# Moving window sums and squares from GpSimd to VectorE, with four plain gate tiles and weights first, in a four-layer fp32 trunk

## The chip, the cores and the metric

The kernel runs on one core of a Trainium2 chip. The metric is the device time of one execution in microseconds. Before the change it is 1521.63 us, the median of three runs (1519.23 to 1524.7).

## The reference

Four pre-norm residual layers over x (512 tokens, 1024 channels, fp32): pool, conv, latent attention (MLA), pool, and a closing RMSNorm. What matters here is the pool layer, and that every product has to be exact to fp32.

```python
POOL_WINDOWS = (2, 4, 8, 16)            # one per group of 512 of the 2048 inner channels

def pool_mixer(xn, w_in, w_grp, scale, w_out):
    u, z = split(xn @ w_in, 2)          # 1024 -> 2 x 2048
    for g, w in enumerate(POOL_WINDOWS):
        mean = (c - prev) / minimum(count_base, w)   # trailing mean of u over w tokens
        pooled.append(mean - u[g])
    mixed = einsum(pooled, w_grp) * scale            # 512 x 512 for each group
    return (mixed * silu(z)) @ w_out                 # 2048 -> 1024

def mla_mixer(...):
    q_lat, kv_lat, k_rope, z = split(xn @ w_in)      # 384, 256, 64, 2048
    q = rms_norm(q_lat) @ w_q_up                     # 16 heads x (128 + 64)
    kv = rms_norm(kv_lat) @ w_kv_up                  # 16 heads x (128 + 128)
    o = causal softmax attention(q, kv, rotated k_rope)
    return (o * silu(z)) @ w_out

for i in range(4):                                   # pool, conv, mla, pool
    x = x + mixer(rms_norm(x), ...)
return rms_norm(x, final_norm)
```

## The kernel before

x lies on the chip as 8 tiles of 128 channels by 512 tokens. A number is held as a high and a low part, each of 32 bits, and a product is three matmuls (high by high, low by high, high by low; lines L257 to L259). Weights come by DMA as raw tiles `wr` of 128x1024 and are split by two steps: `wh` on ScalarE (L244) and `wl` on VectorE (L247). With `pool=True` both stand on GpSimd (L242, L247); that is used for the weights of attention's heads.

Work is a list of **jobs** in a `Stream`. A plain tile (`Layer.tile`, `u..`) is 24 matmuls of 512 columns; a pair (`Layer.pair`, `seven`, `z..`) gives two output tiles at once from sums and differences of weights and of x, with 84 matmuls of 256 columns, and needs eight weight parts in place of four (`ah`, `al`, `sh`, `sl`, `ch`, `cl`, `th`, `tl`; `al`, `sl`, `cl` and `tl` are made on VectorE, L395). The job `m..` mixes a group's channels (24 matmuls), `h0` and `h1` are the halves of the out-projection (tiles `o`). The digits of `u12` are group and tile; `z01` is group 0, second pair. The order of the jobs of the first pool layer is written out by hand:

```python
ORDER = ("u00 u01 u02 u03 u10 u11 u12 u13 z00 z01 m00 m01 z10 z11 " + LATE, ...)
```

While job j runs its matmuls, positions 0 to 7 are counted, and other steps are put at these positions in lists: `prepare(j + 1)`, the weight splits of the next job (a plain tile at positions 1 and 2, a pair at 4 to 7 and 10, 11, where 8 and more means the next job); the post steps of the product before (`post_u`, `post_z`); the forms of x (`XNorm.forms`, the sums and differences that a pair needs, L356 to L381); and sums of squares (`Stats.add`, L281). `Steps.put` (L171) appends, so at one position what was put first goes first. Within `Stream.run` the instructions of TensorE, VectorE and ScalarE stand in exactly this written order, in one in-order queue for each engine. Attention and the first part of the second pool layer lie outside `run`, and there a scheduler sets the order by its own estimates.

`post_u` multiplies a u tile by R (the norm's factor, one row for each token), then makes the trailing sum over w tokens by 1 to 4 shifted adds (`s<-u`, then `s<-s`, 128x513 to 128x527, L608) on GpSimd, then on VectorE the mean and its difference to u (`mean`, three instructions, L615 to L617) at position 12, the high part at 14 on ScalarE and the low part `pll` at 16 on VectorE. A first small memset of the 16 padding columns is GpSimd's (L602). GpSimd also adds squares of x for the norms (L281, all but a layer's last), scales the probabilities p in attention (L1021), and starts some DMAs.

`first_two`, at the end of the kernel, runs u00 and u01 while x still arrives, and R of the first layer comes late: the products up to u11 wait for it in PSUM, and their post steps are drawn into the jobs that follow, up to z00.

## Time and profile before

| what | value |
|---|---|
| median of three runs | 1521.63 us |
| profiled execution | 1516.26 us, span 1514.4 us |
| TensorE, mean granted clock | 0.984 |
| TensorE busy | 1455.7 us (96%), 8632 matmuls |
| VectorE busy | 1096.8 us (72%) |
| ScalarE busy | 677.9 us (45%) |
| GpSimd busy | 324.9 us (21%) |
| DMA | 183.30 MB, mean 121 GB/s |

All times of the trace count from the start of the span of the profiled execution. That execution took 1516.26 us, 5.4 us less than the median of the three runs. A row of the timeline names the start, the length shown, engine, line, operation and the tiles as out<-in; what stands in brackets is the idle time before it and what ended that. The length shown of a VectorE instruction holds some 0.08 us that overlaps with the next one, so the distance of two starts is the better price where instructions follow each other without a wait. In the table of stretches, idle time of an engine is the length less its busy time; PEclk is the granted clock of TensorE as a share of its upper level.

### The profile page before, as it was taken

The page shows a single profiled execution, that of the slowest core. Times are in us where ns is not written, and L with a number is a line of the kernel's source. Part 1 is how long each engine was busy: PE and PEld are TensorE (multiplying, and loading weights), DVE is VectorE, ACT ScalarE, POOL GpSimd, SP SyncE. Part 2 cuts the span into 40 slices and gives each one's busy share as a digit, 9 for nine tenths or more (in the row PEclk, how much of TensorE's full clock was granted, in tenths as well). Part 3 has the DMA queues.
Part 4 walks back from the last instruction along what each step waited for, and adds up shares of the span by engine and source line. Part 5 has one row for each costly group of instructions (what it writes and reads, how often), then busy time and mean ns, then how long its engine had stood idle before and what let it go on. Part 6 is the DMA issues. An engine that isn't in the chain of part 4 may idle for free.

```text
span 1514.4 us, 22602 instructions
## 1 busy us (share of the span) xinstructions
PE 1455.7 (96%) x8632; PEld 1281.9 (85%) x8632; DVE 1096.8 (72%) x1757; ACT 677.9 (45%) x1170; POOL 324.9 (21%) x337
## 2 busy tenths in 40 slices
PE   9799999999999999999989998999999999999997
PEld 7698797887999899999869977888888798888886
DVE  7985557659989879998778867666655487755854
ACT  5353242445555335554455644444633354323333
POOL 2502206021000000000211014355501122310602
PEclk9899999999999999999999999999999999999999
DMA  6353354325676366665236641222122434333431
GB/s 218 89 136 119 88 149 98 126 84 121 180 194 174 126 148 182 173 188 174 84 90 170 169 130 37 69 70 84 43 84 84 111 107 110 129 101 114 123 112 56
DMA packets 66012, 183.30 MB, mean 121 GB/s; under 512 B 8176, under 2 KB 8176, under 8 KB 65904
## 3 DMA queue, kind: packets, MB, share of 16 engines
q1 hardware_dynamic: 57264, 151.97, 31.2%
q0 software_dynamic: 7776, 28.32, 11.4%
q10 hardware_dynamic: 864, 1.57, 0.3%
q8 instruction: 68, 1.11, 0.3%
q14 instruction: 40, 0.33, 0.1%
HBM read 175.27 MB, written 2.10 MB: 117 GB/s over the span
## 4 chain that ended last, share of the span: by engine, by line
PE 68%; DVE 16%; DMA 4%; issue 4%; ACT 4%; POOL 2%; SPq 0%; POOLq 0%; DVEq 0%; ACTq 0%
PE o L259 6%; PE o L257 6%; PE o L258 6%; PE bx L425 5%; PE bx L419 5%; PE bx L424 5%; PE bv L419 3%; PE bv L425 3%; PE bv L424 3%; PE pt L257 3%; PE pt L258 3%; PE pt L259 3%; DMA s<-in_conv_in 2%; DVE wl L247 2%; PE po L258 2%
## 5 line engine op out<-in xcount | busy, mean ns | idle before, releaser
L247 DVE TENSOR_TENSOR wl<-wr,wh 128x1024 fp32r<-128x1024 f32 (+1 forms) x120 | 154.2, 1286 | 52.5 <-ACT wh L244 52.4
L244 ACT ACTIVATE wh<-wr 128x1024 fp32r<-128x1024 f32 (+1 forms) x120 | 125.5, 1048 | 129.9 <-PE o L258 48.2
L259 PE MATMUL o<-yh,wl 128*128 128x512 f32 x384 | 151.6, 395 | 1.9 <-DVE wl L247 1.9
L258 PE MATMUL o<-yl,wh 128*128 128x512 f32 x384 | 151.2, 394 | 0.2 <-DVE yl L656 0.2
L257 PE MATMUL o<-yh,wh 128*128 128x512 f32 x384 | 151.3, 394 | 0.1
L259 PE MATMUL pt<-xh,wl 128*128 128x512 f32 x335 | 132.1, 395 | 4.1 <-DVE wl L247 4.1
L257 PE MATMUL pt<-xh,wh 128*128 128x512 f32 x335 | 132.8, 397 | 2.1 <-ACT xh L347 1.2
L258 PE MATMUL pt<-xl,wh 128*128 128x512 f32 x335 | 132.0, 394 | 0.6 <-DVE xl L348 0.6
L120 POOL DMA_DIRECT2D s<-in_conv_in x30 | 26.0, 868 | 324.4 <-DVE O L459 154.1
L439 ACT ACTIVATE kept<-bv 128x256 f32<-128x256 f32 x54 | 20.7, 384 | 163.5 <-PE bv L425 119.1
L395 DVE TENSOR_TENSOR sl<-s,sh 128x1024 fp32r<-128x1024 f32 x54 | 66.7, 1236 | 30.5 <-ACT sh L392 26.5
L259 PEld LDWEIGHTS o<-yh,wl 128*128 128x128 f32 x384 | 72.1, 188 | 19.5 <-DVE wl L247 2.8
L258 PEld LDWEIGHTS o<-yl,wh 128*128 128x128 f32 x384 | 72.1, 188 | 17.4 <-DVE yl L656 0.5
L257 PEld LDWEIGHTS o<-yh,wh 128*128 128x128 f32 x384 | 72.1, 188 | 16.9 <-ACT yh L653 0.5
L281 POOL TENSOR_TENSOR sq<-sq,sq 128x512 f32<-128x512 f32 x25 | 40.1, 1606 | 210.8 <-ACT sq L275 210.6
L608 POOL TENSOR_TENSOR s<-u 128x527 f32<-128x527 f32 x32 | 48.0, 1501 | 164.9 <-DVE u L579 135.2
L259 PEld LDWEIGHTS pt<-xh,wl 128*128 128x128 f32 x335 | 62.9, 188 | 20.4 <-DVE wl L247 6.1
L257 PEld LDWEIGHTS pt<-xh,wh 128*128 128x128 f32 x335 | 62.9, 188 | 17.5 <-ACT xh L347 2.1
L395 DVE TENSOR_TENSOR al<-wr,ah 128x1024 fp32r<-128x1024 f32 x54 | 66.5, 1232 | 14.5 <-ACT ah L392 12.4
L258 PEld LDWEIGHTS pt<-xl,wh 128*128 128x128 f32 x335 | 62.9, 188 | 15.6 <-DVE xl L348 1.5
L439 ACT ACTIVATE kept<-bx 128x512 f32<-128x512 f32 x108 | 53.0, 490 | 45.6 <-PE bx L425 45.6
L608 POOL TENSOR_TENSOR s<-s 128x525 f32<-128x525 f32 (+2 forms) x48 | 70.0, 1458 | 12.8 <-PE pm L258 9.6
(307 smaller groups left out, 4782.9 us busy)
## 6 DMA issues: line engine op xcount, KB each, us to landing
wr<-in_conv_in SPq DMA_DIRECT2D x34, 512.0 KB, 5.6
wr<-in_pool_out SPq DMA_DIRECT2D x32, 512.0 KB, 3.3
wr<-in_pool_u SPq DMA_DIRECT2D x30, 512.0 KB, 3.5
s<-in_conv_in SPq DMA_DIRECT2D x60, 256.0 KB, 4.5
s<-in_conv_in POOLq DMA_DIRECT2D x30, 512.0 KB, 6.2
wr<-in_pool_z SPq DMA_DIRECT2D x16, 512.0 KB, 4.3
s<-in_pool_z SPq DMA_DIRECT2D x32, 256.0 KB, 3.9
s<-in_pool_z POOLq DMA_DIRECT2D x16, 512.0 KB, 6.0
```

What stands on the lines that cost most here:

```text
L244: nc.scalar.activation(h, raw, AF.Copy)
L247: (nc.gpsimd if pool else nc.vector).tensor_tensor(out=l, in0=raw, in1=f(h), op=ALU.subtract)
L257: nc.tensor.matmul(out, ah, bh, start=first, stop=False)
L258: nc.tensor.matmul(out, ah, bl, start=False, stop=False)
L259: nc.tensor.matmul(out, al, bh, start=False, stop=last)
L281: eng.tensor_tensor(out=self.sum, in0=self.sum, in1=sq, op=ALU.add)
L395: return lambda: nc.vector.tensor_tensor(out=l, in0=t, in1=f(h), op=ALU.subtract)
L419: i = nc.tensor.matmul(out, wh[:, c], xh, start=begin and kk == 0, stop=False, skip_group_check=True)
L424: nc.tensor.matmul(out, wh[:, c], xl, start=False, stop=False, skip_group_check=True)
L425: nc.tensor.matmul(out, wl[:, c], xh, start=False, stop=end and kk == KK - 1, skip_group_check=True)
L439: nc.scalar.activation(dst, src, AF.Copy)
L608: nc.gpsimd.tensor_tensor(out=nx[:, lo:], in0=cur[:, lo:], in1=cur[:, lo - d : S + PAD - d], op=ALU.add)
```

## The change

Eight edits, in the order of the diff:

1. `Steps.put` can put steps ahead of those that stand at a position, and the weight splits of the next job are put so.
2. All sums of squares are VectorE's.
3. In the out-projection the forms of x for the next layer come one job later.
4. In the first pool layer the post steps of the products that wait for R are spread by 6 positions and not by 3.
5. The window sums are VectorE's, one step for each add at positions 2, 3, 4 and 5; mean, high and low follow at 7, 9 and 11 in place of 12, 14 and 16.
6. The first layer's z00 and z01 are four plain tiles with weights in a layout of their own (`pool_z00`), 96 matmuls of 512 columns in place of 168 of 256.
7. The weights of attention's heads are split by ScalarE (high) and VectorE (low), and the last outputs y of attention by VectorE.
8. The forms of the first layer's x come at positions 24 + 16 kk in place of 8 kk.

```diff
-        def put(self, at, by=0):
+        def put(self, at, by=0, first=False):
             for pos, fns in at.items():
-                self.at.setdefault(pos + by, []).extend(fns)
+                l = self.at.setdefault(pos + by, [])
+                l[:] = [*fns, *l] if first else [*l, *fns]
...
-            now.put(self.prepare(j + 1), 2 if self.jobs[j][0] is PAIR ... else 0)
+            now.put(self.prepare(j + 1), 2 if self.jobs[j][0] is PAIR ... else 0, first=True)
...
-                eng = nc.vector if self.i == self.n else nc.gpsimd
-                eng.tensor_tensor(out=self.sum, in0=self.sum, in1=sq, op=ALU.add)
+                nc.vector.tensor_tensor(out=self.sum, in0=self.sum, in1=sq, op=ALU.add)
...
-                    stream.later.put(xn.add(m, wait=8 * (KD - 2 - m + m // 2)))
+                    stream.later.put(xn.add(m, wait=8 * (KD - 1 - m + m // 2)))
...
-        ly = Layer(xn, at, 3 if pre is None else 1)
+        ly = Layer(xn, at, 3 if pre is None else 6)
+        def two_tiles(stream, src, posts, then):
+            for q in range(2):
+                ly.tile(stream, a["pool_z00"][len(zs)], posts[q], then if q else None)
+                zs.append(q)
...
-                    cur, d = u, 1
-                    while d < w:
-                        nx = up.tile([P, S + PAD], F32, tag="u", name=nm("s"))
-                        lo = 2 * d - 1
-                        nc.gpsimd.tensor_tensor(out=nx[:, lo:], in0=cur[:, lo:], in1=cur[:, lo - d : S + PAD - d], op=ALU.add)
-                        cur, d = nx, 2 * d
-                    sums.append(cur)
+                    sums.append(u)
+                def add(d):
+                    cur, nx = sums[0], up.tile([P, S + PAD], F32, tag="u", name=nm("s"))
+                    lo = 2 * d - 1
+                    nc.vector.tensor_tensor(out=nx[:, lo:], in0=cur[:, lo:], in1=cur[:, lo - d : S + PAD - d], op=ALU.add)
+                    sums[0] = nx
...
-                return {0: [mul], 12: [mean], 14: [high], 16: [low]}
+                adds = {2 + q: [lambda q=q: add(2**q)] for q in range(g + 1)}
+                return {0: [mul], **adds, 7: [mean], 9: [high], 11: [low]}
...
-                z_[g, i] = lambda ...: ly.pair(stream, wz[2 * g + i], (post_z, post_z), mid and mid(g, i))
+                z_[g, i] = lambda ...: (ly.pair if g or pre is None else two_tiles)(stream, wz[2 * g + i], (post_z, post_z), mid and mid(g, i))
...
-            wh, wl = wchunk(wv[g], pool=True)
+            wh, wl = wchunk(wv[g])
...
-            wh, wl = wchunk(wq[8 + g], 768, pool=True)
+            wh, wl = wchunk(wq[8 + g], 768)
...
-                hold["q"] = wchunk(wq[h // 2], 768, pool=True)
+                hold["q"] = wchunk(wq[h // 2], 768)
...
-                hold["k"] = wchunk(wk[h // 4], pool=True)
+                hold["k"] = wchunk(wk[h // 4])
...
-                    split_y(nc.gpsimd)
+                    split_y()
...
-            s1.later.put(xn0.forms(kk), 8 * kk)
+            s1.later.put(xn0.forms(kk), 24 + 16 * kk)
```

Where instructions move shows at three places. In the names, `u` is a product times R, `s` a window sum, `hd` and the two instructions after it are the mean, `pll` the low part; `wl` is the low part of a plain tile's weights, `al`, `sl`, `cl` of a pair's; `sz` a gate tile.

First place: VectorE's queue at the start of the first layer, around the first gate products. Before:

```order
L616 SCALAR_TENSOR_TENSOR s_510<-s_510,u_479 128x512
L617 TENSOR_TENSOR s_510<-hd_600,u_479 128x16
L615 TENSOR_TENSOR hd_608<-s_517,con 128x16
L616 SCALAR_TENSOR_TENSOR s_517<-s_517,u_482 128x512
L617 TENSOR_TENSOR s_517<-hd_608,u_482 128x16
L395 TENSOR_TENSOR al_574<-wr_497,ah_573 128x1024
L615 TENSOR_TENSOR hd_618<-s_525,con 128x16
L616 SCALAR_TENSOR_TENSOR s_525<-s_525,u_485 128x512
L617 TENSOR_TENSOR s_525<-hd_618,u_485 128x16
L395 TENSOR_TENSOR sl_578<-s_132_499,sh_577 128x1024
```

and with the change, ahead of the weight split of z01's first tile (the lines count from the changed file: L616 the window sum, L622 to L624 the mean, L630 the low part, L248 `wl`):

```order
L616 TENSOR_TENSOR s_600<-u_440 128x527
L630 TENSOR_TENSOR pll_439<-s_550,plh_438 128x512
L622 TENSOR_TENSOR hd_613<-s_595,con 128x16
L623 SCALAR_TENSOR_TENSOR s_595<-s_595,u_563 128x512
L624 TENSOR_TENSOR s_595<-hd_613,u_563 128x16
L579 TENSOR_TENSOR u_443<-pt_326,R_427 128x512
L579 TENSOR_TENSOR sz_620<-pt_570,R_427 128x512
L622 TENSOR_TENSOR hd_635<-s_600,con 128x16
L623 SCALAR_TENSOR_TENSOR s_600<-s_600,u_440 128x512
L624 TENSOR_TENSOR s_600<-hd_635,u_440 128x16
L248 TENSOR_TENSOR wl_624<-wr_566,wh_623 128x1024
L616 TENSOR_TENSOR s_644<-u_443 128x527
```

Before, a pair's splits stood between the means; with the change window sums, products with R and low parts stand between them, and one split of a plain tile comes after them.

Second place: VectorE's queue ahead of z30, the last but one pair of the first layer. Before:

```order
L247 TENSOR_TENSOR wl_2209<-wr_2157,wh_2208 128x1024
L579 TENSOR_TENSOR u_2248<-pt_2210,R_475 128x512
L615 TENSOR_TENSOR hd_2293<-s_2220,con 128x16
L616 SCALAR_TENSOR_TENSOR s_2220<-s_2220,u_2197 128x512
L617 TENSOR_TENSOR s_2220<-hd_2293,u_2197 128x16
L395 TENSOR_TENSOR al_2260<-wr_2200,ah_2259 128x1024
L650 SCALAR_TENSOR_TENSOR E_1919<-pm_2267,par,E_1919 128x512
L395 TENSOR_TENSOR sl_2264<-s_414_2202,sh_2263 128x1024
```

and with the change:

```order
L616 TENSOR_TENSOR s_2165<-u_2136 128x527
L630 TENSOR_TENSOR pll_2084<-s_2121,plh_2083 128x512
L616 TENSOR_TENSOR s_2171<-s_2165 128x525
L616 TENSOR_TENSOR s_2180<-s_2171 128x521
L395 TENSOR_TENSOR al_2148<-wr_2085,ah_2147 128x1024
L616 TENSOR_TENSOR s_2187<-s_2180 128x513
L660 SCALAR_TENSOR_TENSOR E_1803<-pm_2155,par,E_1803 128x512
L395 TENSOR_TENSOR sl_2152<-s_402_2087,sh_2151 128x1024
```

The mean that stood ahead of `al` (and waited for GpSimd's sums) has moved behind `sl`; three window sums of the last u tile have come ahead of `al`, and the fourth between `al` and `sl`.

Third place: VectorE's queue in attention, at the rotary part of one group of heads (`t`, `qr`, `qal`, `qbl`). Before:

```order
L971 TENSOR_TENSOR t_1682_9699<-qr_9685,cos 128x512
L972 TENSOR_TENSOR t_1683_9700<-qr_9697,sin 128x512
L975 TENSOR_TENSOR qr_9685<-qr_9685,sin 128x512
L973 TENSOR_TENSOR t_1682_9699<-t_1682_9699,t_1683_9700 128x512
L1049 TENSOR_TENSOR O_8125<-po_9735,O_8125 128x512
L974 TENSOR_TENSOR t_1683_9700<-qr_9697,cos 128x512
L161 TENSOR_TENSOR qal_9708<-t_1682_9699,qah_9707 128x512
L976 TENSOR_TENSOR t_1683_9700<-t_1683_9700,qr_9685 128x512
L161 TENSOR_TENSOR qbl_9712<-t_1683_9700,qbh_9711 128x512
```

and with the change:

```order
L981 TENSOR_TENSOR t_1670_9583<-qr_9569,cos 128x512
L248 TENSOR_TENSOR wl_9753<-wr_9750,wh_9752 128x768
L985 TENSOR_TENSOR qr_9569<-qr_9569,sin 128x512
L982 TENSOR_TENSOR t_1671_9584<-qr_9581,sin 128x512
L1059 TENSOR_TENSOR O_8009<-po_9619,O_8009 128x512
L983 TENSOR_TENSOR t_1670_9583<-t_1670_9583,t_1671_9584 128x512
L984 TENSOR_TENSOR t_1671_9584<-qr_9581,cos 128x512
L248 TENSOR_TENSOR wl_9759<-wr_9756,wh_9758 128x1024
L986 TENSOR_TENSOR t_1671_9584<-t_1671_9584,qr_9569 128x512
L161 TENSOR_TENSOR qal_9592<-t_1670_9583,qah_9591 128x512
L248 TENSOR_TENSOR wl_9985<-wr_9982,wh_9984 128x768
L161 TENSOR_TENSOR qbl_9596<-t_1671_9584,qbh_9595 128x512
```

Three weight splits that were GpSimd's stand now among the nine instructions.

## Rows read from the trace of the kernel before

**Rows 1.** The page: busy time, share and count by engine; one group.

```profile
PE 1455.7 (96%) x8632; PEld 1281.9 (85%) x8632; DVE 1096.8 (72%) x1757; ACT 677.9 (45%) x1170; POOL 324.9 (21%) x337
...
L244 ACT ACTIVATE wh<-wr 128x1024 fp32r<-128x1024 f32 (+1 forms) x120 | 125.5, 1048 | 129.9 <-PE o L258 48.2
```

**Rows 2.** What TensorE waited for in the whole run: total us, times, longest.

```profile
PE bx L425 <- DVE tl L395: 8.4, 9, 2.9
...
PE s L1007 <- ACT kh L158: 5.5, 2, 4.9
```

**Rows 3.** Nine stretches: length, busy us by engine, PEclk, DMA share, GB/s.

```profile
42.41:100.49 58.08, 49.15 (x265) 43.54 (x264) 53.73 (x79) 26.08 (x41) 20.60 (x23) 0.85 0.43 110
153.00:163.00 10.00, 7.81 (x31) 5.24 (x30) 9.11 (x13) 2.84 (x4) 5.34 (x5) 1.00 0.17 54
254.00:280.00 26.00, 22.96 (x174) 22.22 (x173) 23.92 (x33) 13.04 (x22) 6.63 (x5) 0.93 0.44 131
338.00:373.00 35.00, 31.98 (x178) 26.70 (x177) 30.94 (x62) 19.72 (x31) 3.35 (x4) 1.00 0.50 113
753.00:771.00 18.00, 14.09 (x56) 9.97 (x55) 14.57 (x30) 8.27 (x14) 0.77 (x1) 1.00 0.25 80
815.00:871.00 56.00, 52.59 (x420) 51.30 (x419) 48.41 (x85) 33.47 (x58) 5.85 (x6) 0.97 0.66 163
892.00:958.00 66.00, 57.84 (x280) 48.13 (x279) 42.13 (x96) 27.77 (x70) 26.68 (x27) 0.90 0.28 79
958.00:1100.00 142.00, 136.98 (x760) 117.89 (x759) 90.16 (x249) 72.77 (x194) 71.30 (x80) 1.00 0.20 60
1265.00:1440.00 175.00, 169.82 (x947) 147.22 (x946) 116.61 (x151) 63.29 (x92) 48.91 (x44) 0.99 0.40 114
```

**Rows 4.** GpSimd's groups: busy us, mean ns, idle before and its releasers.

```profile
L608 POOL TENSOR_TENSOR s<-s 128x525 f32<-128x525 f32 (+2 forms) x48 | 70.0, 1458 | 12.8 <-PE pm L258 9.6
L608 POOL TENSOR_TENSOR s<-u 128x527 f32<-128x527 f32 x32 | 48.0, 1501 | 164.9 <-DVE u L579 135.2 <-ACT xtok L1168 23.3 <-DVE s L617 3.6
L281 POOL TENSOR_TENSOR sq<-sq,sq 128x512 f32<-128x512 f32 x25 | 40.1, 1606 | 210.8 <-ACT sq L275 210.6
L247 POOL TENSOR_TENSOR wl<-wr,wh 128x768 fp32r<-128x768 f32 (+1 forms) x16 | 34.7, 2170 | 1.3
```

**Rows 5.** VectorE's timeline, 16 to 33 us: start, length, instruction.

```profile
20.42 1.51 DVE L363 SCALAR_TENSOR_TENSOR d<-x,par,g 128x256 f32<-128x256 f32 x1
...
30.60 0.48 DVE L362 SCALAR_TENSOR_TENSOR d<-x,par,g 128x256 f32<-128x256 f32 x1
31.00 0.48 DVE L363 SCALAR_TENSOR_TENSOR d<-x,par,g 128x256 f32<-128x256 f32 x1
```

**Rows 6.** GpSimd's timeline, two rows between 16 and 75 us.

```profile
18.47 6.06 POOL L281 TENSOR_TENSOR sq<-sq,sq 128x512 f32<-128x512 f32 x4 [0.61 <-ACT sq L275]
...
49.89 1.07 POOL L608 TENSOR_TENSOR s<-u 128x527 f32<-128x527 f32 x1
```

**Rows 7.** VectorE's timeline, 53 to 75 us.

```profile
57.27 1.21 DVE L395 TENSOR_TENSOR al<-wr,ah 128x1024 fp32r<-128x1024 f32 x1
58.40 1.03 DVE L615 TENSOR_TENSOR hd<-s,con 128x16 f32<-128x16 f32 x1
...
65.99 0.69 DVE L623 TENSOR_TENSOR pll<-s,plh 128x512 fp32r<-128x512 f32 x1
66.59 0.17 DVE L615 TENSOR_TENSOR hd<-s,con 128x16 f32<-128x16 f32 x1
...
67.62 0.68 DVE L579 TENSOR_TENSOR u<-pt,R 128x512 f32<-128x512 f32 x1
```

**Rows 8.** TensorE's timeline where z01 ends and m00 begins.

```profile
89.31 0.28 PE L425 MATMUL bx<-fh,sl 128*128 128x256 f32 x1
89.43 0.39 PE L257 MATMUL pm<-plh,wh 128*128 128x512 f32 x1
89.66 0.40 PE L258 MATMUL pm<-pll,wh 128*128 128x512 f32 x1
```

More of the change, by code (lines that the diff above doesn't have):

```diff
@@ L218, in step @@
             now, self.later = self.later, Steps()
-            now.put(self.prepare(j + 1), 2 if self.jobs[j][0] is PAIR and self.jobs[j + 1 :] and self.jobs[j + 1][0] is not PAIR else 0)
+            now.put(self.prepare(j + 1), 2 if self.jobs[j][0] is PAIR and self.jobs[j + 1 :] and self.jobs[j + 1][0] is not PAIR else 0, first=True)
             self.jobs[j][2](self.ready.pop(j, None), now)
@@ L623, in low, with post_z @@
                     nc.vector.tensor_tensor(out=l, in0=sums[0][:, PAD:], in1=f(h), op=ALU.subtract)
-                return {0: [mul], 12: [mean], 14: [high], 16: [low]}
-            def post_z(t, sign, szs=szs):
+                adds = {2 + q: [lambda q=q: add(2**q)] for q in range(g + 1)}
+                return {0: [mul], **adds, 7: [mean], 9: [high], 11: [low]}
+            def post_z(t, sign, szs=szs, plain=g == 0 and pre is not None):
+                sz = ut("sz") if plain else t
                 def scale():
-                    tmul(t, t, ly.R[sign])
+                    tmul(sz, t, ly.R[sign])
                 def gate():
-                    nc.scalar.activation(t, t, AF.Silu)
-                    szs.append(t)
+                    nc.scalar.activation(sz, sz, AF.Silu)
+                    szs.append(sz)
                 return {0: [scale], 3: [gate]}
@@ L664, in pool_layer @@
             for i in range(2):
-                z_[g, i] = lambda g=g, i=i, post_z=post_z: ly.pair(stream, wz[2 * g + i], (post_z, post_z), mid and mid(g, i))
+                z_[g, i] = lambda g=g, i=i, post_z=post_z: (ly.pair if g or pre is None else two_tiles)(stream, wz[2 * g + i], (post_z, post_z), mid and mid(g, i))
                 m_[g, i] = lambda mix=mix, i=i: mix(i)
@@ L1324, in _layout @@
         out[f"pool_u{j}"] = w_in(i["pool_w_in"][j][:, :DI])
+        if j == 0:
+            out["pool_z00"] = w_in(i["pool_w_in"][j][:, DI : DI + 4 * P])
         out[f"pool_z{j}"] = w_pair(i["pool_w_in"][j][:, DI:])
```

1 line of the change is left out of this document (added).

## The prediction

> **What bounds the kernel now.** I read first the busy times of the engines [rows 1]. TensorE (PE) is busy for 1455.7 of 1514.4 us, VectorE for 1096.8, ScalarE for 677.9, GpSimd for 324.9. TensorE is the bound, and what any edit elsewhere can give is what TensorE loses: 58.7 us in which it stands idle, and the stretches in which its granted clock is the lower of its two levels (1.2 against 2.4 GHz). Next I read for what it waits [rows 2]: VectorE's weight splits of a pair (tl, 8.4 us) and ScalarE's kh in attention (5.5 us) stand at the head, and nearly all other waits are for splits too. So the losses are late operands. Third, I cut the run by stretches [rows 3]: length less TensorE's busy time is 8.93 us in the first row, then 2.19, 3.04, 3.02, 3.91, 3.41, 8.16, 5.02 and 5.18: 42.9 of the 58.7 us lie in nine stretches, and the clock column (0.85, 0.93, 0.97, 0.90 in four of them) shows what the lower level costs on top. Outside them the rest of the idle time is the load of x and the end of the run, which the change hardly touches.
>
> Why the operands are late shows on VectorE. In the first microseconds one 256-element instruction takes 1.51 us; the same kind takes 0.48 a little later [rows 5]. In the slow case GpSimd runs four adds back to back [rows 6]; in the fast one it runs none. So a VectorE instruction can be held by a GpSimd add for about the length of that add, and GpSimd runs 80 window sums, 25 sums of squares and 16 weight splits of this kind, of 1.46 to 2.17 us [rows 4]. The Trainium skill (SBUF — State Buffer, Who interferes with whom) says that a VectorE instruction with two SBUF inputs and a GpSimd instruction that reads SBUF contend for one port pair, which the first holds for its whole instruction while the other is blocked. The 1.51 against 0.48 us agree; by that rule alone all waits of this kind would go with the GpSimd work, which is the third rival below. But the fifth stretch has 3.91 us of idle TensorE with GpSimd busy for 0.77 [rows 3], so there it is VectorE's order, not contention.
>
> **The change part by part.** *Prices.* VectorE starts a 512-element add or split 0.60 us after the last, a 1024-element split takes 1.13, a mean (three instructions) 1.03 [rows 7], a 256-element form 0.40 [rows 5]. The window sums have 513 to 527 elements; VectorE has none before, so I take 0.60 by its nearest rows and keep 1.07, what such a sum takes on GpSimd when nothing disturbs it [rows 6], as the upper end. TensorE needs 0.12 us per matmul of 256 columns and 0.23 per one of 512 [rows 8]: a pair (84) 9.9 us, a plain tile (24) 5.53.
>
> *What moves to VectorE:* 80 sums x 0.60 = 48 us, 25 sums of squares x 0.60 = 15, 16 splits of attention's weights at 0.85 or 1.13, about 16, and 12 splits y x 0.60 = 7. That is 86 us on an engine with 418 us free; the question is only where it is not free. It loses the waits behind GpSimd, and its 28 splits do not cost GpSimd anything any more. ScalarE gets 16 casts of about 1.05 us [rows 1], with half of its time free in attention (72.77 of 142 busy, [rows 3]).
>
> *Term 1, start of the first layer (first stretch).* VectorE is busy for 53.73 of 58.08 us here, so it sets the pace together with TensorE, and the work must be counted. In the new order 66 VectorE instructions stand from the first product with R to the weight split of z01's second tile: 32 of about 512 elements (19.2 us), 7 means (7.2), 5 weight splits (5.7) and 8 forms (3.2), 35.3 us, and with 0.2 for the longer sums 35.5. R comes just ahead of u12, which began at 42.41 [rows 3]; from 42.3 us they are done at 77.8, with 1 us for instructions that wait for the one before at 78.8. TensorE, starting u12 some 0.7 us earlier than before (41.7, since the forms of x that stood ahead come later), would begin that tile at 41.7 + 5 x 5.53 + 0.5 = 69.9 and use the split at its third matmul, 70.4. It is 8.4 us late in sum. So this wait stays: not four waits behind al, sl and tl, but two or three behind wl. Then z01's second tile and m00, m01 follow, and z10 begins at 78.8 - 0.5 + 3 x 5.53 = 94.9, where it began at 100.49. Two pairs that become four tiles cost 22.1 - 19.8 = 2.3 us of this, and it is included. The lower clock level came after waits of 3 to 4 us here; the waits that stay are as long, but a slow tile gives VectorE time to catch up: 2.8 us. Gain 2.8; bounds 0 (the clock takes all of the 5.6) and 5.5 (nearly none).
>
> *Term 2, out-projection of the first half (153 to 163).* The split of o's weights waits behind a split and means that GpSimd holds; with no adds there and weights first, VectorE's work per tile is 5.9 us at most (four sums, mean, product, splits) against 5.53 for a u tile and 3.7 for a mixing job: two u and one m take 14.8 us, VectorE about 15 at group 3 and less at group 2. It fits within the slack of the mixing splits. Of 2.19 idle I take 2.2, for 1.5 to 2.7.
>
> *Term 3, the last pair of the first layer (254 to 280).* Idle 3.04 and clock 0.07 x 26 = 1.8. The last u job has four sums, which now stand on VectorE ahead of al; counting the new order from the start of m21 at these prices I get al at 253.4 where TensorE wants it at 254.7, and sl and tl within 0.3 us. Taken 4.5, for 3.0 to 4.9.
>
> *Terms 4 and 5, starts of conv and of attention's input (338 to 373, 753 to 771).* Weights go ahead of sums and forms, and the forms come one job later; 3.02 and 3.91 us idle. Behind the weights the sum of squares closes about 0.6 us later per form moved, which may cost a new wait of 0.5 to 1 us at the first pair. Taken 2.7 (1.5 to 3.5) and 4.2 (3.4 to 4.9).
>
> *Term 6, attention's gate pairs (815 to 871).* Idle 3.41, clock 0.03 x 56 = 1.7. Weights first helps tl here, but the statistics of the latents stay in front. Taken 2.3, for 0.8 to 3.8.
>
> *Term 7, attention.* 892 to 958: idle 8.16, clock 0.10 x 66 = 6.6. The k weights that GpSimd split in 2.17 us come from VectorE in 1.13, and the rotary chain of one group, in which three instructions wait behind such splits, gets some 3 us shorter, though three splits now stand in it. Taken 6.0, for 2 to 11. 958 to 1100: idle 5.02, of which those waits go where the scaling of p is queued behind splits on GpSimd; 3.0, for 0 to 4. Against it 0.7 for the ScalarE casts that stand ahead of qh and kh. A cast there waits until TensorE gives the weights' buffer back, and qh, kh and th are queued behind it; this is where the change adds a wait.
>
> *Term 8, the second pool layer (1265 to 1440).* Idle 5.18, clock 0.01 x 175 = 1.8: the two pairs whose al, tl and kept stand behind sums. Taken 5.2, for 1.5 to 6.9.
>
> *Term 9, new small waits.* In the u jobs of both pool layers VectorE's margin shrinks to a microsecond or less, each first sum now waits for GpSimd's memset of the padding, and behind it stand the next weight splits. Taken -1.5, for -5 to 0.
>
> *At nothing:* the conv layer's own pairs and the end of the run keep their order; GpSimd's DMAs of pairs get earlier, with DMA at 0.4 to 0.6.
>
> *Sum.* 2.8 + 2.2 + 4.5 + 2.7 + 4.2 + 2.3 + 6.0 + 3.0 - 0.7 + 5.2 - 1.5 = 30.7 us. The profiled execution took 1516.26 us (span 1514.4), so it would take 1485.6. The median of the runs is 5.4 us above the profiled one, and I carry this over: 1521.6 - 30.7 = 1491. The low ends give 8 us, the high ends 47.
>
> **The rivals.**
> *VectorE becomes the bound in the pool layers.* If a sum of 527 elements takes 1.07 us on VectorE, the 12 sums of term 1 cost 5.6 more, and terms 2, 3 and 8 halve (-5.9): a gain of 19.2, 1502. For it: 53.73 busy of 58.08. Against it: an add takes 0.60 at 512. The Trainium skill (Perfetto Trace Analysis, Optimizing Scalar/DVE Operations) says that with VectorE saturated it may make sense to move work off to ScalarE or GpSimd; the change does the reverse in that very stretch, and this rival is what the rule would mean here.
> *The waits come back as others.* VectorE is free earlier, but TensorE then waits for ScalarE's half of the split, for a DMA or for kept: half of the sum, 1506. For it: kh and kept are among the waits now. Against it: ScalarE is at 45%.
> *All closes.* Every wait of the nine stretches goes and the clock stays up: 45 us, 1476. Against it: the count of term 1.
> *Slower, through attention's splits.* 16 casts of 1.05, 16 splits of about 1 and 12 of 0.6 are 40 us. If all lay on the chain from one head's scores to the next, term 7 would turn from 8.3 to -40, and the sum to -18: 1539. It decides once more than 22 of the 40 us lie on that chain, which is what the other terms give. Against it: VectorE is busy for 90.16 of 142 us there, and GpSimd's versions already stood ahead of the same matmuls, longer.
> *No change:* gains and new waits cancel, 1521.
>
> **How the numbers follow.** Forecast 0.55 (1491), VectorE bound 0.14 (1502), waits come back 0.13 (1506), all closes 0.11 (1476), no change 0.03, slower 0.04. From 1476 to 1508 the range holds all but the last two and the worst corner of the forecast. A measurement of this kernel tells some 0.3% (4.6 us) from no change; by that: faster 0.93, same 0.03, slower 0.04.
>
> **What would show it.** Term 1: z10's first matmul near 97 to 98 us, waits there for wl only, VectorE almost without a gap from 42 to 79. Sums on VectorE of 0.6 to 0.7 us, and no VectorE instruction of 512 elements over 1.5 us outside attention. The pair at 254 takes 10 us and not 15. Conv's and attention's first tiles follow one another. In attention the rotary chain is shorter by 3 us. VectorE's busy time up by less than 86 us, GpSimd's down by some 200. The forecast is wrong if a sum takes 1 us, if ScalarE's casts hold kh, or if TensorE runs longer at the lower clock.

## The result, and the profile after

| | before | after |
|---|---|---|
| median of four runs each | 1520.43 us | 1503.92 us (1499.83 to 1506.29) |
| ratio, 95% interval | | 0.9888 (0.9852 to 0.9924) |
| profiled execution, span | 1516.26, 1514.4 us | 1506.29, 1504.5 us |
| second profiled execution, span | 1514.97, 1513.1 us | 1502.15, 1500.4 us |

The change makes the kernel 16.5 us faster (interval 11.6 to 22.5), about half of the 30.7 us forecast. The two pairs of profiled executions differ by 9.9 and 12.7 us in span, so the table of stretches below has to explain some 11 us; the first profiled execution of the changed kernel is the slowest of its four runs.

The page after: busy time, share and count of each engine.

```profile
PE 1452.4 (97%) x8560; PEld 1274.9 (85%) x8560; DVE 1114.8 (74%) x1876; ACT 686.7 (46%) x1174; POOL 100.4 (7%) x186
```

Against [rows 1]: VectorE took over some 86 us of work, by the prediction's count, and is busy only 18 us longer (1114.8 for 1096.8). The kinds of VectorE instruction that both kernels have became shorter by some 61 us in all (the first of a mean, 128x16, from 0.45 to 0.17 us on average), and four tiles need fewer splits than two pairs. GpSimd fell by 224.5 us. TensorE has 72 matmuls fewer, and is idle for 52.1 in place of 58.7 us.

What TensorE waited for in the whole run after: total us, times, longest.

```profile
PE pt L260 <- DVE wl L248: 8.9, 5, 3.2
PE bv L419 <- ACT kept L439: 8.4, 3, 4.9
PE bx L425 <- DVE tl L395: 5.6, 9, 1.0
...
PE s L1017 <- ACT kh L158: 3.1, 3, 2.0
...
PE pj L1044 <- POOL p L1031: 0.7, 1, 0.7
```

Against [rows 2]: tl fell from 8.4 to 5.6 us and kh from 5.5 to 3.1, but **kept**, a copy of a product that ScalarE makes in the middle of a pair, has come up with 8.4 us in only three waits, the longest 4.9, and wl stands at the head.

The stretches of [rows 3] after, cut near the same jobs: length, busy us of TensorE, weight load, VectorE, ScalarE, GpSimd (instructions), granted clock, DMA share, GB/s.

```profile
42.10:97.60 55.50, 48.42 (x194) 38.08 (x192) 49.83 (x88) 24.53 (x36) 2.05 (x4) 0.94 0.29 79
150.40:160.40 10.00, 7.29 (x28) 4.80 (x28) 9.86 (x17) 4.31 (x6) 0.00 (x0) 1.00 0.16 52
252.00:274.00 22.00, 20.92 (x172) 20.38 (x171) 18.48 (x29) 11.68 (x20) 0.00 (x0) 1.00 0.52 158
...
376.40:500.60 124.20, 121.24 (x1010) 119.42 (x1009) 110.45 (x157) 67.84 (x113) 10.22 (x17) 1.00 0.67 177
...
876.50:958.00 81.50, 77.37 (x395) 65.35 (x394) 58.11 (x140) 44.10 (x103) 10.30 (x20) 0.96 0.28 81
958.00:1090.00 132.00, 128.27 (x700) 109.79 (x699) 95.43 (x246) 75.78 (x188) 22.61 (x44) 1.00 0.21 62
1254.00:1426.00 172.00, 165.22 (x902) 142.81 (x901) 118.07 (x176) 62.15 (x91) 4.26 (x12) 0.98 0.39 114
```

Idle TensorE (length less busy) is 7.1 us in the start, 2.7 in the out-projection, 1.1 at the last pairs of the first layer (3.04 before), 3.0 in twelve conv pairs, 4.1 and 3.7 in attention (8.16 and 5.02 before; these two rows begin and end 2 to 11 us away from the work of [rows 3], and cut after the same matmuls, 887.4 to 946.8 and 946.8 to 1088, the idle time is again 4.1 and 3.7), and 6.8 in the second pool layer (5.18 before). From the starts of the jobs in the two profiles of each kernel follow the lengths of the stretches:

| stretch, from job to job | before, 2 profiles | after, 2 profiles | forecast | measured gain |
|---|---|---|---|---|
| u12 to z10 (term 1, its start 0.3 to 0.7 earlier) | 58.1, 58.2 | 55.5, 56.6 | 2.8 | 2.2 to 2.9 |
| first two tiles of the out-projection (2) | 14.4, 14.4 | 14.9, 14.9 | 2.2 | -0.5 |
| last two pairs, first layer (3) | 25.1, 24.9 | 21.5, 21.6 | 4.5 | 3.4 |
| first conv tile to first pair (4) | 27.0, 27.0 | 23.5, 23.5 | 2.7 | 3.5 |
| first two conv pairs | 21.1, 21.0 | 23.7, 23.7 | 0 | -2.6 |
| the other 28 conv pairs | 281.2, 283.0 | 287.8, 285.1 | 0 | -4.4 |
| attention's input to first gate pair (5) | 39.6, 39.6 | 36.5, 36.5 | 4.2 | 3.1 |
| gate pairs (6) | 88.3, 85.9 | 86.7, 84.8 | 2.3 | 1.4 |
| attention to the second pool layer (7) | 305.3, 304.1 | 297.6, 297.8 | 8.3 | 7.0 |
| second pool layer up to its first out-projection (8) | 139.6, 138.9 | 137.5, 137.5 | 5.2, with the next | 1.8 |
| its last two pairs (8) | 22.6, 22.5 | 27.7, 26.5 | | -4.6 |

The gains sum up to some 10.5 us, so 20 of the 30.7 us forecast are missing in the stretches (14 in the medians). The starts of the first pool layer, of conv and of attention's input, the first layer's last pairs and attention itself won what they should within a third, and four lines lost: the out-projection, the conv pairs in two places, and the last pairs of the second layer.

### The profile page after: what moved, and what is told of

Same layout as the page of the kernel before. It is cut to its first block, busy times and chain, and to the rows that moved or that the text cites. A ratio compares the mean times of both kernels' runs of the same rounds, so it can differ in the third digit from the quotient of the medians.

```text
span 1504.5 us, 22342 instructions
## 1 busy us (share of the span) xinstructions
PE 1452.4 (97%) x8560; PEld 1274.9 (85%) x8560; DVE 1114.8 (74%) x1876; ACT 686.7 (46%) x1174; POOL 100.4 (7%) x186
## 5 line engine op out<-in xcount | busy, mean ns | idle before, releaser
L245 ACT ACTIVATE wh<-wr 128x1024 fp32r<-128x1024 f32 (+1 forms) x140 | 144.6, 1035 | 168.1 <-PE o L259 50.9
L248 DVE TENSOR_TENSOR wl<-wr,wh 128x1024 fp32r<-128x1024 f32 (+1 forms) x140 | 167.8, 1199 | 59.7 <-ACT wh L245 59.3
L260 PE MATMUL pt<-xh,wl 128*128 128x512 f32 x367 | 146.1, 399 | 8.9 <-DVE wl L248 8.9
L260 PE MATMUL o<-yh,wl 128*128 128x512 f32 x384 | 151.2, 394 | 2.3 <-DVE wl L248 2.3
L258 PE MATMUL pt<-xh,wh 128*128 128x512 f32 x367 | 146.8, 400 | 1.6 <-ACT wh L245 0.8
L259 PE MATMUL pt<-xl,wh 128*128 128x512 f32 x367 | 146.2, 398 | 0.0
L260 PEld LDWEIGHTS pt<-xh,wl 128*128 128x128 f32 x367 | 69.8, 190 | 27.3 <-DVE wl L248 11.1
L258 PEld LDWEIGHTS pt<-xh,wh 128*128 128x128 f32 x367 | 70.0, 191 | 18.1 <-ACT wh L245 1.5
L392 ACT ACTIVATE sh<-s 128x1024 fp32r<-128x1024 f32 x52 | 54.9, 1056 | 32.1 <-DMA s<-in_conv_in 13.4
L419 PE MATMUL bv<-xh,ch 128*128 128x256 f32 x208 | 59.4, 286 | 8.4 <-ACT kept L439 8.4
L392 ACT ACTIVATE ah<-wr 128x1024 fp32r<-128x1024 f32 x52 | 54.6, 1050 | 27.8 <-issue 12.0
L425 PE MATMUL bx<-fh,tl 128*128 128x256 f32 x208 | 60.1, 289 | 5.6 <-DVE tl L395 5.6
```

Source lines behind the costliest of these rows:

```text
L245: nc.scalar.activation(h, raw, AF.Copy)
L248: (nc.gpsimd if pool else nc.vector).tensor_tensor(out=l, in0=raw, in1=f(h), op=ALU.subtract)
L258: nc.tensor.matmul(out, ah, bh, start=first, stop=False)
L259: nc.tensor.matmul(out, ah, bl, start=False, stop=False)
L260: nc.tensor.matmul(out, al, bh, start=False, stop=last)
L392: return lambda: nc.scalar.activation(h, t, AF.Copy)
```

## The experiments

Each ratio is to runs of the kernel before on the same chip. The experiments ran on four chips, so a few microseconds between two totals tell little, and the places in the traces decide. Edits 2 (sums of squares) and 4 (the spread of the post steps) were never undone alone; what they are worth is not shown. The parts are told by what they settle; the names in brackets are used further down.

**The changed kernel and the kernel before once more** (a_same, b_same), unedited.

> The changed kernel once more, for a second profile. Theory: what it lost against the forecast are waits set by its own order. The first half's out-projection shows again some 3.3 us of waits at its first two tiles (before: 2.7), the last pair but one of the second pool layer again 15 us or more in place of 10, and the conv layer's pairs again take 9 us more than before. Rival: the conv layer's part is chance of one execution (late transfers of weights); then the 32 conv pairs of this profile differ by several us from the 334 us or so of the first one, while the other two places stay.

> The kernel before once more, for a second profile of it. Theory: its conv pairs take again some 322 us for 32. Rival (chance of late transfers): they differ from the first profile by 3 us or more, and the waits of its pairs stand at other pairs.

Measured: 1502.89 us (ratio 0.9889, 0.9859 to 0.9919), and 1514.97 us for one execution of the kernel before. Nine of the eleven lines of the table repeat within 1.2 us in both kernels, five of them within 0.2. The widest of the nine are the start (55.5, 56.6) and the last two pairs of the second layer (27.7, 26.5) after the change. The other two are the gate pairs (2 us apart) and the 28 conv pairs, which differ by 2 to 3 us within each kernel, nearly all slow pairs standing at other places each time. So out-projection and last pairs are set by the order, and in the conv pairs chance has a part; what part is told at the end.

**One tile more on the chip** (buffer71). The tiles of 512 tokens (x, its forms, u, sums, parts of y) share one pool of 70.

```diff
-NU = 70
+NU = 71
```

> The changed kernel with 71 in place of 70 tiles of 512 tokens on the chip. Theory: the first half's out-projection begins late because a window sum on VectorE waits for a tile that TensorE has still to read, and the weight split stands behind it in VectorE's queue: the 6.4 us of idle VectorE ahead of it shrink by half or more, the first two tiles of the out-projection take 14.1 us or less in place of 14.9, total 1 to 2 us less. Rival: VectorE is simply late with its own work there; no change at that place.

VectorE's timeline of the changed kernel, where the first half's out-projection begins (150.69): start, length, idle before and what ended it.

```profile
141.53 0.70 DVE L616 TENSOR_TENSOR s<-u 128x527 f32<-128x527 f32 x1
148.59 1.51 DVE L616 TENSOR_TENSOR s<-s 128x525 f32<-128x525 f32 x2 [6.35 <-PE pm L259]
...
151.16 0.68 DVE L579 TENSOR_TENSOR u<-pt,R 128x512 f32<-128x512 f32 x1
151.76 1.22 DVE L248 TENSOR_TENSOR wl<-wr,wh 128x1024 fp32r<-128x1024 f32 x1
```

and the same place with 71 tiles (out-projection from 153.12):

```profile
143.96 0.70 DVE L616 TENSOR_TENSOR s<-u 128x527 f32<-128x527 f32 x1
144.70 1.44 DVE L616 TENSOR_TENSOR s<-s 128x525 f32<-128x525 f32 x2
...
147.76 0.69 DVE L579 TENSOR_TENSOR u<-pt,R 128x512 f32<-128x512 f32 x1 [0.48 <-PE pt L260]
148.37 1.22 DVE L248 TENSOR_TENSOR wl<-wr,wh 128x1024 fp32r<-128x1024 f32 x1
```

The second window sum of a u tile stands idle for 6.35 us until a matmul of the mixing job (pm) is through: it needs a free tile, and the one it gets is still read by TensorE. The mean, the next product and wl, the weights that TensorE wants at 151.2, are queued behind it and come at 151.76. With one more tile the sum follows at once, wl starts 4.7 us ahead of the out-projection, and its first two tiles take 11.1 us, which is their plain length, in place of 14.9. The total is 1499.03 us (0.9867, 0.9829 to 0.9906), too wide to tell 3.8 us by itself; the place tells them.

**Means late** (mean_late). The last group's mean, high and low part five positions later, sums unmoved.

```diff
-                return {0: [mul], **adds, 7: [mean], 9: [high], 11: [low]}
+                late = 5 if g == 3 else 0
+                return {0: [mul], **adds, 7 + late: [mean], 9 + late: [high], 11 + late: [low]}
```

> The changed kernel with mean, high and low part of the last group's u tiles five positions later (12, 14 and 16 as before); the sums stay where they are. Theory: the pair after the last mixing job loses its time since ScalarE's high part of the mean stands ahead of the copy of a product that TensorE waits for, and itself waits for VectorE: the pair of the second pool layer takes 10 to 13 us and not 17.7, the one of the first layer 10 and not 11.6, total 4 to 9 us less. Rival: the splits of the pair are late by themselves; then the wait stays and only changes its name.

ScalarE's timeline in the changed kernel, at the pair that took 17.8 us:

```profile
1413.84 0.61 ACT L663 ACTIVATE yh<-E 128x512 fp32r<-128x512 f32 x1
...
1418.95 0.63 ACT L627 ACTIVATE plh<-s 128x512 fp32r<-128x512 f32 x1 [4.50 <-DVE s L624]
1419.49 0.36 ACT L439 ACTIVATE kept<-bv 128x256 f32<-128x256 f32 x1
```

and TensorE's there:

```profile
1419.91 0.58 PE L419 MATMUL bv<-xh,ch 128*128 128x256 f32 x1 [4.86 <-ACT kept L439]
```

and ScalarE's at the same place with the means late:

```profile
1408.86 0.62 ACT L664 ACTIVATE yh<-E 128x512 fp32r<-128x512 f32 x1
1409.75 0.38 ACT L439 ACTIVATE kept<-bv 128x256 f32<-128x256 f32 x1 [0.28 <-PE bv L425]
```

plh, the high part of the mean, stands ahead of kept in ScalarE's queue. It waits 4.50 us for VectorE, which does the sums of the last two u tiles and the pair's splits first; kept, for which nothing is missing but the engine, goes at 1419.49, and TensorE stands 4.86 us. With the mean late kept waits 0.28 us for its product, and the two pairs take 20.9 us; those of the first layer 20.8 in place of 21.5. The total is 1498.12 us (0.9865, 0.9836 to 0.9894), 4.8 less than the changed kernel on the same chip. The theory holds; the rival (late splits) would have left the wait in place.

**Pairs kept** (pairs_kept). z00 and z01 as pairs, with the forms of x where they were.

```diff
-            def post_z(t, sign, szs=szs, plain=g == 0 and pre is not None):
+            def post_z(t, sign, szs=szs, plain=False):
...
-                z_[g, i] = lambda ...: (ly.pair if g or pre is None else two_tiles)(...)
+                z_[g, i] = lambda ...: ly.pair(...)
...
-            s1.later.put(xn0.forms(kk), 24 + 16 * kk)
+            s1.later.put(xn0.forms(kk), 8 * kk)
```

> The changed kernel with z00 and z01 as pairs again, and the forms of x of the first layer at 8 kk again, which they need. Theory: VectorE sets the pace here and gets the pairs' splits and forms on top of the sums, so the stretch from u12 to z10 takes 59 to 63 us in place of 56, with waits behind al, sl and tl; total 3 to 7 us more. Rival: without GpSimd adds the pairs' splits come in time, and 2.3 us of TensorE are saved: 53 to 55 us.

The stretch from u12 to z10 here, and what TensorE waited for in it:

```profile
42.93:93.18 50.25, 44.07 (x265) 38.16 (x264) 46.88 (x83) 22.59 (x37) 2.68 (x9) 1.00 0.45 118
```

```profile
PE bv L419 <- ACT kept L439: 4.2, 2, 2.6
PE bx L425 <- DVE tl L395: 1.1, 1, 1.1
```

50.25 us in place of 55.5 and 56.6: the theory fell and the rival was right, by more than it said. VectorE is busy for 46.88 us and not 49.83, although it makes the pairs' splits; TensorE stands idle for 6.2 us, beside 7.1 and 8.7 in the changed kernel, it saves the 2.3 us of the wider tiles, and its clock stays at the upper level (1.00 against 0.94 in both profiles of the changed kernel). Not all of the 5 to 6 us is the pairs' gain. In the three later kernels with pairs and weights first (best_three, copy_first and forms_early, below) the same stretch takes 50.3 to 52.6 us, and in all four the next one, from z10 to the out-projection, takes 54.5 to 54.7 us in place of 53.1. From u12 to the out-projection the four take 104.9 to 107.1 us, where five profiles with the four tiles and the new order (the changed kernel twice, buffer71, mean_late, attn_gpsimd) take 108.5 to 109.7. So the four plain tiles cost some 3 us where the rest of the change had already made the pairs fast. (To this rest belongs the spread of edit 4. In the first layer it is by 6 positions in place of 1, and not of 3: `3 if pre is None else 1` gives 1 there.) The total is 1499.25 us (0.9859, 0.9823 to 0.9896), not told from the changed kernel's by itself.

**Window sums back on GpSimd** (sums_gpsimd), inside the product's step, with means at 12, 14 and 16; all else as changed.

> The changed kernel with the window sums back on GpSimd, inside the product's step, and mean, high and low at 12, 14 and 16 as before; sums of squares, attention's splits, four plain tiles and weights first stay as changed. Theory (a GpSimd add holds VectorE for its length): the first layer's last but one and last pair take 23 to 25 us in place of 21.5, VectorE shows instructions of 1.5 to 2.4 us again, but the pair of the second layer takes 12 to 13 in place of 17.7 since its means come late again; total -3 to +3. Rival (VectorE's own load costs more than the contention): 4 us faster or more, the start of the first layer included.

VectorE's timeline at the last pairs of the first layer in that kernel:

```profile
255.78 0.18 DVE L628 TENSOR_TENSOR hd<-s,con 128x16 f32<-128x16 f32 x1 [5.02 <-POOL s L615]
255.99 1.50 DVE L629 SCALAR_TENSOR_TENSOR s<-s,u 128x512 f32<-128x512 f32 x1
...
258.36 1.21 DVE L395 TENSOR_TENSOR al<-wr,ah 128x1024 fp32r<-128x1024 f32 x1
...
261.49 1.76 DVE L395 TENSOR_TENSOR cl<-wq,ch 128x512 fp32r<-128x512 f32 x1
```

and GpSimd's beside it:

```profile
257.02 5.68 POOL L615 TENSOR_TENSOR s<-s 128x525 f32<-128x525 f32 x3
```

The picture of the kernel before is back: VectorE waits 5.02 us for a sum of GpSimd, a product of 512 elements then takes 1.50 and a split 1.76 us while GpSimd runs, and the last two pairs take 25.8 us in place of 21.5. From z10 to the out-projection and in its first two tiles some 2 us more are lost (54.0 and 15.9 for 53.1 and 14.9). But the start from u12 is 53.8 us where the changed kernel has 55.5 and 56.6 (in one profile, at a granted clock of 0.97 against 0.94), and the last pairs of the second layer 23.8 in place of 27. In total 1500.97 us, 1.9 less than the changed kernel's second measurement and within the noise of it. The largest edit of the change, engine and positions taken together, is thus neutral as it stands: what contention gives back the new places of the steps take. The run undoes both at once and does not price the engine alone.

**Attention's splits back on GpSimd** (attn_gpsimd).

```diff
-            wh, wl = wchunk(wv[g])
+            wh, wl = wchunk(wv[g], pool=True)
...
-                    split_y()
+                    split_y(nc.gpsimd)
```

(and likewise the q and k weights)

> The changed kernel with attention's weight splits and the last twelve splits of y back on GpSimd, nothing else. Theory: from the second rotary product's stretch to the second pool layer (pa to the first tile of that layer) attention takes 304 us as in the kernel before, against 297.7 us with the change: 6 to 7 us more in total, with TensorE waiting for kh and p again. Rival: the gain of attention came from elsewhere (weights first, the state of the clock); then it stays at 298 to 300.

What TensorE waited for in attention, with the splits on GpSimd:

```profile
PE s L1017 <- ACT kh L158: 5.5, 2, 4.9
PE pj L1044 <- POOL p L1031: 3.9, 4, 1.5
PE pk L260 <- DVE wl L248: 2.3, 1, 2.3
```

and in the changed kernel:

```profile
PE s L1018 <- DVE kl L161: 3.3, 4, 1.3
PE s L1017 <- ACT kh L158: 3.1, 3, 2.0
PE pj L1044 <- POOL p L1031: 0.7, 1, 0.7
```

302.8 us for the stretch, against 297.6 and 305.3: 5.2 of the 7 us are this edit's. kh, p and the k weights are the waits that go, kl comes up by 1.7. The rotary chain (first product with cos to the split of qb) takes 9.5 us, where it took 11.75; three splits stand in it now, at 0.87 and 1.14 us. kh hangs on this chain: in ScalarE's queue qh and kh stand behind qbh, and qbh waits for the chain's last product. Before, and in the changed kernel:

```profile
940.80 0.63 ACT L158 ACTIVATE qbh<-t 128x512 fp32r<-128x512 f32 x1 [4.74 <-DVE t L976]
```

```profile
928.66 0.63 ACT L158 ACTIVATE qbh<-t 128x512 fp32r<-128x512 f32 x1 [0.70 <-DVE t L986]
```

With the splits back on GpSimd it is 4.74 us again. The wait that I had named is there too, a cast that stands 2.66 us for a matmul on the q weights with qah and qbh behind it:

```profile
925.64 1.06 ACT L245 ACTIVATE wh<-wr 128x1024 fp32r<-128x1024 f32 x1 [2.66 <-PE pq L259]
926.61 0.61 ACT L158 ACTIVATE qah<-t 128x512 fp32r<-128x512 f32 x1
```

**Weights last** (weights_last). Weight splits behind the other steps of a position again.

```diff
-            now.put(self.prepare(j + 1), ..., first=True)
+            now.put(self.prepare(j + 1), ...)
```

> The changed kernel with the next job's weight splits put behind the other steps of a position again. Theory: the starts of conv and of attention's input lose what they won: the stretch from the first conv tile to the first conv pair 25 to 27 us in place of 23.5, from attention's first input tile to its first gate pair 38 to 39.6 in place of 36.5; total 4 to 7 us more. Rival: the later forms and VectorE's sums of squares did it; then both stay within 1 us of the changed kernel.

First conv tile to first pair 24.5 us (23.5), attention's input 38.2 (36.5), the first layer from z10 to the out-projection 55.5 (53.1). So of terms 4 and 5 (3.5 and 3.1 us) weights first gives 0.9 and 1.7 in these stretches; by exclusion the later forms and the rest give the remainder there. The total of 1505.82 us is 1.9 to 2.9 above the changed kernel, less than the 4 to 7 of the theory, and not told from noise.

**Three edits together** (best_three): pairs, late means, 71 tiles.

> The changed kernel with z00 and z01 as pairs (and the first layer's forms at 8 kk), the last group's means late, and 71 tiles on the chip: three edits that each won at a place of its own. Theory (the three causes are independent): u12 to z10 about 50 us, the first half's first two out-projection tiles about 11 to 12 us, the last pairs 20.8 us in both pool layers, in sum 5.5 + 3.5 + 0.7 + 6 = 15 us less than the changed kernel, some 1488 us. Rival (a freed wait is taken over by the next one): 5 to 8 us less, 1495 to 1498.

1489.27 us, ratio 0.9795 (0.9772 to 0.9819): faster than both kernels, by 13.6 us than the changed kernel's second measurement. Start 52.6 us (50.3 when the pairs alone were kept: here the lower clock came in), out-projection tiles 11.1, last pairs 20.8 and 20.9. The theory of independent causes holds, with 15 us forecast and about 14 measured, though the start gave less than its 5.5.

**The copy first** (copy_first), on top of these three.

```diff
-        now(1)
         q = product(w, xf, "S1", "N1", V, begin=True)
         snap(part(0), V)
+        now(1)
```

> The kernel best_three with ScalarE's first copy of a product in every pair put ahead of the other steps of position 1. Theory: in the first conv pair the copy waits since a step that itself waits for VectorE stands ahead of it in ScalarE's queue, so that pair goes from 13.0 to 12.0 us or less, and attention's gate pairs lose the wait of 2.6 us for a copy: 1 to 4 us less than best_three. Rival: these pairs wait for VectorE's al and tl anyway; then the copy comes earlier and the pairs stay.

1488.45 us, the first conv pair 13.0 as before: the rival was right there, TensorE waits 1.0 us each for VectorE's al and tl and 0.3 for kept. In attention's gate pairs the wait for kept did not go either; it is 2.3 us here, where best_three has 1.1 and the changed kernel 2.5 and 1.5. Why it is so long stays open.

**Forms early** (forms_early), on top of the three.

```diff
-                    stream.later.put(xn.add(m, wait=8 * (KD - 1 - m + m // 2)))
+                    stream.later.put(xn.add(m, wait=8 * (KD - 2 - m + m // 2)))
```

> The kernel best_three with the forms of x in the out-projections one job earlier, as before the change. Theory: the later forms moved the wait from the first conv tiles into the first conv pair (13.0 us and not 10.4), so that pair falls to 10.4 to 11 us, while the stretch from the first conv tile to it grows from 23.5 to 25 or 26 us, and attention's from 36.5 to 38; in sum within 1.5 us. Rival: weights first alone keeps the tiles at 23.5 and 36.5, and 2.6 us are won.

The conv stretch in this kernel, and in the changed one (first tile to first pair, then two pairs):

```profile
321.61:348.39 26.78, 25.21 (x101) 19.85 (x100) 23.75 (x53) 14.14 (x22) 3.33 (x4) 0.94 0.42 96
348.39:368.79 20.40, 20.04 (x169) 19.84 (x168) 19.24 (x27) 12.05 (x20) 0.98 (x2) 1.00 0.68 168
```

```profile
329.24:352.77 23.53, 23.43 (x101) 18.71 (x100) 20.47 (x49) 13.15 (x21) 3.22 (x4) 1.00 0.42 107
352.77:376.44 23.67, 20.89 (x169) 20.07 (x168) 23.36 (x33) 13.51 (x23) 1.09 (x3) 1.00 0.62 144
```

47.2 us in both: in conv the later forms move the wait from the tiles into the pairs and win nothing. Attention's input takes 37.8 us with the early forms and 36.5 with the late ones, so there they win 1.2. The total of 1490.01 us is not told from best_three's.

**Weights last, on top of the three** (three_weights_last).

> The kernel best_three with weight splits behind the other steps again. What it tells: in the kernels with weights first the 28 conv pairs after the first two took 283.3 to 288.3 us in ten profiles, in the three without (the kernel before twice, weights_last) 280.7 to 283.0, although the order of the conv pairs is the same in both. Theory (weights first costs the conv pairs some 4 us): 283 us or less here, while the starts of conv and attention and the first layer lose 2 to 5 us, total within 3 us of best_three. Rival (chance of late transfers): 284 to 288 us, and the total is 2 to 5 us above best_three.

The 28 conv pairs took 288.2 us, so weights first is not what makes them long; of the rival, chance was right. Over 14 profiles they took 280.7 to 288.3 us, the kernel before 281.2 and 283.0 in two. The slow pairs come where ScalarE waits for a transfer of the pair's second weights:

```profile
592.52 1.06 ACT L392 ACTIVATE sh<-s 128x1024 fp32r<-128x1024 f32 x1
...
602.15 0.38 ACT L439 ACTIVATE kept<-bx 128x256 f32<-128x256 f32 x1 [0.69 <-PE bx L425]
605.45 1.06 ACT L392 ACTIVATE sh<-s 128x1024 fp32r<-128x1024 f32 x1 [2.91 <-DMA s<-in_conv_in]
```

The cast of s goes some 7.7 us after a pair's start when all is well; here it waits 2.91 us for the DMA, and the pair that needs these weights takes 12.1 us in place of 9.9. Over the 14 profiles such waits of the cast (0.15 us or more) add up to 3.6 to 13.4 us, and the length of the 28 pairs follows them (correlation 0.95): the seven profiles with over 10 us of them took 285.1 to 288.3 us, the other seven 280.7 to 286.1. So the spread goes with transfers that come late; no run changes the transfers to test it. The order of the instructions in them is the same in all kernels. Whether the kernels after the change have more of these waits than the kernel before (4.1 to 13.4 us in twelve profiles, 3.6 and 8.3 in two) stays open.

The total is 1498.88 us, 9.6 above best_three and more than either theory said: start 55.4 in place of 52.6 (at a granted clock of 0.91 and 0.94), out-projection 12.4 in place of 11.1, conv and attention inputs 0.9 and 1.7 longer as before, gate pairs 3.2 longer (over 14 profiles they vary from 84.4 to 88.3). Beside pairs, weights first is worth more than it showed alone (here about 7 of the 9.6 us lie in stretches that the order sets, the clock's part in them included).

## Why the prediction was right and where it was not

Direction and range were right; the size was 1.9 times too large. The measured 1503.92 us lies where two rivals had their price (1502 and 1506) and not at the 1491 of the forecast. The first of them did not come: a window sum takes 0.62 us on VectorE and not 1.07. The second came in part, as told under term 8. By its steps:

*Contention.* Right. VectorE has 22 and 21 instructions of 512 elements over 1 us in the two profiles before and 2 in each after; 15 are there with the window sums back on GpSimd, 9 with attention's splits back. The two that stay (1.76 and 1.77 us in the first profile, from 1474 to 1478) run beside four multiplications of GpSimd near the end of the kernel. A window sum on VectorE costs what I took: 80 of them, 0.70 us as shown, 0.62 apart.

```profile
L616 DVE TENSOR_TENSOR s<-s 128x525 f32<-128x525 f32 (+2 forms) x48 | 33.5, 699 | 7.2 <-PE pm L259 6.4
...
L616 DVE TENSOR_TENSOR s<-u 128x527 f32<-128x527 f32 x32 | 22.5, 702 | 0.5
```

The Trainium skill (SBUF — State Buffer, Who interferes with whom) gives a port pair held for a whole instruction as the cause. These counts agree, though in sums_gpsimd the larger part of a stop is VectorE waiting for the sum itself (5.02 us).

*Term 1* hit the number (z10 at 97.6 and 98.3; forecast 97.7) by the count of VectorE's work and waits for wl alone (7.1 us). It failed as a statement on the change: I counted the four tiles as a cost of 2.3 us within a gain and did not count the same stretch with pairs. With pairs the stretch takes 50.3 to 52.6 us, so the rest gains 5.5 to 8 us there, and the tiles take more than half of it back (some 3 us up to the out-projection). The Trainium skill (Perfetto Trace Analysis, Optimizing Scalar/DVE Operations) has the rule that I had weighed as a rival, moving work off VectorE where it is saturated; the same passage adds that between these two engines it might not help. sums_gpsimd decides neither way: its start is 1.7 to 2.8 us shorter, at a higher clock, and about 1 us of it is lost again up to the out-projection.

*Term 2* failed in its first step. I added up VectorE's work per tile and compared it with TensorE's, and left out what VectorE waits for. The sum takes a tile from a pool that is empty at that time, and it is TensorE's matmuls of the mixing job that give one back. The row was on the table: [rows 4] shows GpSimd's sums idle for 12.8 us, 9.6 of them until pm. At this very place GpSimd waited 5.97 us in the kernel before, where VectorE now waits 6.35:

```profile
151.56 2.20 POOL L608 TENSOR_TENSOR s<-s 128x525 f32<-128x525 f32 x2 [5.97 <-PE pm L258]
```

GpSimd could afford that wait, since nothing urgent stood behind it. In VectorE's queue the weights stand behind it, and buffer71 takes it away. In place of 2.2 us won, 0.5 were lost.

*Term 3* was right in kind (3.4 for 4.5); 0.7 of the missing 1.1 us is the wait for kept, as mean_late shows.

*Terms 4 and 5.* 3.5 for 2.7 and 3.1 for 4.2, but "may cost a new wait of 0.5 to 1 us at the first pair" was 2.6 in conv: forms_early shows that there the later forms only move the wait.

*Term 6.* 1.4 for 2.3, in a stretch that varies by 4 us from one execution to the next: not told.

*Term 7* was right: 7.0 for 8.3, its mechanism confirmed by undoing it (5.2). The rotary chain became 2.2 us shorter and not 3.

*Term 8* failed: 5.2 forecast, -2.8 measured. Of the two waits for kept that I counted on to go, that at the layer's first pairs went (2.69 us at 1274.85 before, none after; the stretch won 1.8), and that at its last two pairs grew from 0.91 to 4.86 us. I asked what stands ahead of VectorE's splits, not what stands ahead of ScalarE's copies once the means move five positions forward; mean_late shows that it was this. In the words of the rivals: the second one ("the waits come back as others", with kept named as the sign) held in this place, for 8 of the 20 us that are missing in the stretches. The 2.7 missing in the out-projection are an exchange of the same kind, but for a tile, which that rival had not named.

*At nothing:* the 28 conv pairs lost 4.4 us between the pairs of profiles, a stretch in which no instruction moves. Their length follows the transfers that come late, and it was not in the range of any term.

*Term 9* had the sign and, at -1.5 us, was too small for what it stood for: the new waits were not many small ones but two large ones, each behind an instruction that waits at the head of an in-order queue.

*The rival "All closes"* was added up wrong: its 45 us hardly exceed the 42.9 us of idle time alone, and counting the clock as the terms do (8.7 + 1.8 + 1.7 + 6.6 + 1.8 us) gives 63. The measured gain is far from either.

## What to carry to other kernels

When work moves from an engine with slack to one whose queue feeds the bound, price not only its duration but each thing that it waits for (a buffer, a cast, another engine), and list what is queued behind it: the waits that the old engine bore for nothing become the bound's. Read the idle column of the instructions that move; it names those waits. And judge the parts of a change one at a time: here the largest part was neutral, one cost some 3 us, and two small corrections (one tile more, late means) gave some 11 us at their places, beside 16.5 for the whole change.

## What the runs showed of the hardware that I had not expected

In the start stretch the granted clock is 0.94 in both profiles of the changed kernel, with three waits for wl of 1.33 to 4.11 us, and 1.00 with pairs kept, where the two longest waits were 1.62 and 2.56 us. In best_three, with the same pairs and waits of 1.64 and 2.56 us, it fell once, to 0.94 over the stretch. The same order of instructions thus runs at either level, and the stretch takes 50.25 or 52.60 us. And 28 conv pairs whose instructions do not change take 280.7 to 288.3 us from one execution to the next, by when the transfers of their weights land.
